# Five groups of elementwise work move from POOL to DVE, and transposes get 40 places of priority, in a one-core fp32 kernel of two transformer blocks

## The chip, the cores and the metric

The kernel runs on one core of one Trainium2 chip. A core has a matrix engine (PE), a vector engine (DVE), a scalar engine (ACT), a general engine (POOL) and a queue engine (SP), each of which takes its own instructions in the order in which they stand. The metric is the device time of one execution in microseconds (us), as the median of several runs; lower is better.

## The reference

The input is 512 tokens of width 1024 with a context of 256 tokens, all in fp32. Two blocks of two layers each run one after the other; the output is the tokens after the second.

```
# first block, each of two layers
h = rms_norm(x) * (1 + scale) + shift ;  p = h @ w_in ;  p_ctx = h_ctx @ w_in
layer 0: q, k = apply_rope(rms_norm(heads(p))), y_a = softmax attention over context and all tokens
         y_b = hyena_branch: two long convolutions with generated taps,
               taps = taps * rsqrt(sum(taps * taps, axis=0) + EPS)
layer 1: y_w = windowed attention (q, k with rope) ;  y_n = neighbourhood attention (8 x 16 keys per token)
y = concat(y_1 * silu(gate_1), y_2 * silu(gate_2)) ;  x = x + gate * (y @ w_out)

# second block, each of two layers
merged = sigmoid(x @ w_g0) * (o_nsa @ w_br_nsa) + sigmoid(x @ w_g1) * (o_mla @ w_br_mla)
       + sigmoid(x @ w_g2) * (o_fox @ w_br_fox)
x = layer_norm(a * x + merged @ w_out)
x = layer_norm(a * x + cross_attention(x, mem))
x = layer_norm(a * x + square(relu(x @ w_up)) @ w_down)

def apply_rope(x, cos, sin):      # pairs (x0, x1) of a head
    return stack([x0 * cs - x1 * sn, x0 * sn + x1 * cs])
```

## The kernel before

**Tiles.** Tokens stand in tiles of 128 rows. Every product that must be exact is made of three matmuls in the reduced form fp32r: each operand is split into a high and a low part (`split`, L54 on ACT writes the high part, L55 the low part, by a subtraction on DVE or on the engine that `eng` names), and `mm3` (L81 to L83) adds high x high, high x low and low x high in PSUM. Weights come by DMA to a staging tile and are split on their way into a tile `u` (`wu`, L1178).

**Transposes.** `tr` (L86) transposes a 128x128 block on PE through an identity matrix into the PSUM tag `pt`; ACT and DVE copy the result out and split it.

**Stages.** In the first block, `gqa_proj` projects q, k and v of an attention. Each pair of 128-token tiles goes through `head_norm`: a square on ACT (L255), sums of squares on DVE (L256), the inverse root in nine small DVE instructions (L63 to L76), the scaling (L259), and, where there is a rope, four strided products with the sine on POOL (L270), one product with the cosine on DVE (L272) and the sum of the two on DVE (L273), whose result PE transposes. In layer 0 this projection runs alone; in layer 1 it runs beside other work. The hyena filters' taps are made in `hy_taps`: the squares of a block (L549 on ACT) are added up (L550 on POOL) and summed over partitions by a matmul with ones (L555). `gates` multiplies an attention's output by silu of its gate: a tanh, a product on DVE out of PSUM (L757) and a product on POOL (L759). `nat_proj` (L898 on) projects for the neighbourhood attention and has its weights split on POOL (L902); `neigh` is that attention, where the probabilities are transposed, copied out by ACT (L1023) and multiplied with the values (L1026). `out_proj` adds its output on POOL (L778), which stays so.

In the second block, three attentions run beside the `branch` generator: a gate projection, a branch projection, a product on DVE out of PSUM (L1672) and, for the second and third branch, an addition to `merged` on POOL (L1673).

**Order.** Stages are generators; `mix` draws from two of them in turn, by the costs that they yield, so that attention and projections alternate in the program. A scheduler then sets each engine's order at build time: among instructions whose operands come in order it takes the one of the highest priority, which is the place in the program, unless a `high_priority` block moves it ahead by its offset. PSUM has two tiles of the tag `mm`, three of `S`, two of `pt` and one of `o`; in SBUF `u` and `st` have four tiles each, `e` six and `va` four.

In the names below, `e`, `a`, `u`, `sm` and so on are these tags; numbers behind them count the tiles.

Of the kernel before, what the change touches and what calls it, by code (L numbers as in the profile page):

```python
# [12 lines left out]
OP = mybir.AluOpType  # L13
AF = mybir.ActivationFunctionType
AX = mybir.AxisListType
P = 128
# [11 lines left out]
class Net:  # L28
# [54 lines left out]
        mm(ps, al, bh, start=False, stop=last)  # L83

    def tr(self, dst, src, n=P):
        self.nc.tensor.transpose(dst, src, self.ident[:n, :n])  # L86


    def q_pair(self, ps, A, B, n, scale=None):
# [158 lines left out]
    def head_norm(self, p, nh, gain, rope=None, tag='v2'):  # L248

        nc = self.nc  # L250
        n = 2 * nh * 64
        sq = self.t(tag, [P, 512])[:, :n]
        q = self.t(tag, [P, 512])[:, :n]
        ss = self.t('sm', [P, 2 * nh])
        nc.scalar.activation(sq.rearrange("p (i c) -> p i c", i=2), p, AF.Square)  # L255
        nc.vector.tensor_reduce(ss, sq.rearrange("p (h d) -> p h d", d=64), axis=AX.X, op=OP.add)  # L256
        r = self.rsqrt(ss, 2 * nh, 1.0 / 64, 1e-6).rearrange("p (i h) -> p i h", i=2)
        q4 = q.rearrange("p (i h d) -> p i h d", i=2, d=64)
        nc.vector.tensor_tensor(q4, p.rearrange("p i (h d) -> p i h d", d=64), bc(r[:, :, :, None], [P, 2, nh, 64]), op=OP.mult)  # L259
        if rope is None:  # L260
            q3 = q.rearrange("p (h d) -> p h d", d=64)
            nc.vector.tensor_tensor(q3, q3, bc(gain[:, None, :], [P, 2 * nh, 64]), op=OP.mult)
            return q
        cs, sn = rope
        qo = q.rearrange("p (i h c two) -> p i h c two", i=2, c=32, two=2)
        to = sq.rearrange("p (i h c two) -> p i h c two", i=2, c=32, two=2)
        so = sn.rearrange("p i (c two) -> p i c two", two=2)
        for i in range(2):
            for e in range(2):
                nc.gpsimd.tensor_tensor(to[:, i, :, :, e], qo[:, i, :, :, 1 - e], bc(so[:, i, None, :, e], [P, nh, 32]),  # L270
                                        op=OP.mult)
        nc.vector.tensor_tensor(q4, q4, bc(cs[:, :, None, :], [P, 2, nh, 64]), op=OP.mult)  # L272
        nc.vector.tensor_tensor(q, q, sq, op=OP.add)  # L273
        return q
# [240 lines left out]
    def hy_taps(self, o, hf, ni, w3, C):  # L515
# [13 lines left out]
        for b in range(nb):  # L529
            d = C['dec'][b // 2][:, b % 2, ch]  # L530
            ps = self.ps('S')
            for j in range(2):
                c = slice((b0 + b) * P, (b0 + b + 1) * P)
                p = ps[:, j * 256:(j + 1) * 256]
                nc.tensor.matmul(p, hs[:, c], wh[:, j, ch], start=True, stop=False)
                nc.tensor.matmul(p, hs[:, c], wl[:, j, ch], start=False, stop=b > 0)
                if b == 0:

                    for m in range(2):
                        for ww in (wh, wl):  # L540
                            nc.tensor.matmul(p, self.h0[:, (m + j + 1) % 2], ww[:, m, ch], start=False,
                                             stop=m == 1 and ww is wl)
            v = self.t('va', [P, 2, 256])
            nc.vector.tensor_tensor(v, ps.rearrange("p (j c) -> p j c", j=2), bc(d[:, None, :], [P, 2, 256]), op=OP.mult)
            if b == 0:
                nc.scalar.activation(acc, v, AF.Square)
            else:
                q = self.t('va', [P, 2, 256])
                nc.scalar.activation(q, v, AF.Square)  # L549
                nc.gpsimd.tensor_tensor(acc, acc, q, op=OP.add)  # L550
            self.split(E[b][:, 0], E[b][:, 1], v)
            yield 2.2
        ps = self.ps('o')[:, :256]
# [191 lines left out]
    def gates(self, w, i0, streams, order, fill=False):  # L745

        nc = self.nc
        for m in order:
            u = self.wu(w, i0 + m)
            for h, nt, y in streams:  # L750
                n = nt * P
                ps = self.ps('mm')[:, :n]
                self.pT(ps, u, h, slice(0, n))
                th = self.t('v2', [P, 512])[:, :n]
                nc.scalar.activation(th, ps, AF.Tanh, scale=0.5)
                yt = y[m // 2][:, m % 2]
                nc.vector.scalar_tensor_tensor(yt if fill else th, th, 1.0, ps, op0=OP.add, op1=OP.mult)  # L757
                if not fill:
                    nc.gpsimd.tensor_tensor(yt, yt, th, op=OP.mult)  # L759
                yield 5.2 * nt / 4  # L760

    def out_proj(self, w, y, nt, xs, gate, each):
# [134 lines left out]
    def nat_proj(self, streams, gain):  # L897

        nc = self.nc
        for i0, what in ((10, 'k'), (14, 'v'), (6, 'q')):  # L900
            for c in range(2):
                us = [self.wu('w1', i0 + 2 * c + k, eng=nc.gpsimd) for k in range(2)]  # L902
                cs = slice(c * 256, (c + 1) * 256)
                for h, nt, ctx in streams:
                    if what == 'q' and ctx:
# [745 lines left out]
    def branch(self, l, b, gi, o, x, merged, first=False):  # L1651
# [4 lines left out]
        for m in range(8):  # L1656
# [12 lines left out]
            if first:  # L1669
                nc.vector.scalar_tensor_tensor(d, g, 1.0, ps, op0=OP.add, op1=OP.mult)  # L1670
            else:
                nc.vector.scalar_tensor_tensor(g, g, 1.0, ps, op0=OP.add, op1=OP.mult)  # L1672
                nc.gpsimd.tensor_tensor(d, d, g, op=OP.add)  # L1673
            yield 5.2 + nk * .65

    def run(self, *gens):
# [539 lines left out]
```

## Time and profile before

| | |
|---|---|
| median of 3 runs | 2979.03 us (2976.75, 2979.03, 2984.97) |
| profiled run | 2982.7 us, of which the span is 2980.6 us |
| PE busy | 2817.7 us, 95% of the span |
| DVE busy | 1947.7 us, 65% |
| ACT busy | 1380.4 us, 46% |
| POOL busy | 262.4 us, 9% |
| TensorE's granted clock, mean | 0.982 of full speed |

The span runs from the first to the last instruction of the profiled execution; what lies around it is start and end of the run. Busy time is the time in which an engine had at least one instruction at work. A matmul's own time in a row is longer than the step to the next one, because matmuls overlap; the step is read from two starts. An idle time in square brackets stands before the row's instruction, with the instruction whose end ended it.

### The profile page before, as it was taken

The numbers are of one execution on the slowest core, as the hardware profiler recorded it, in microseconds if no ns is written. First come the engines' busy times: TensorE is split into PE (matmuls) and PEld (weight loads), VectorE is DVE, ScalarE is ACT, GpSimd is POOL, SyncE is SP. The second block draws the span as 40 slices with busy tenths as digits, with TensorE's granted clock in tenths as the row PEclk, the third lists the DMA queues.
The fourth block names the chain that finished last, engine by engine and source line by source line (L and its number), as shares of the span: only waits on it lengthen the run. The fifth ranks groups of instructions, "written<-read, shape, count | busy, mean of one in ns | idle before, by whom it ended". The sixth has DMA issues, their size and how long they took to land.

```text
span 2980.6 us, 40408 instructions
## 1 busy us (share of the span) xinstructions
PE 2817.7 (95%) x14904; PEld 2285.3 (77%) x14904; DVE 1947.7 (65%) x4339; ACT 1380.4 (46%) x2843; POOL 262.4 (9%) x310
## 2 busy tenths in 40 slices
PE   7898899889899899999999899999999999899998
PEld 3788757558888778777788788887787778788886
DVE  5767768885777756976756843436787663954335
ACT  5543566343365634655543522324465552633222
POOL 0212100101211310100110000000100011000000
PEclk8999999899999999999999999999999999999999
DMA  6433133653214332312124232323221124223221
GB/s 226 136 121 98 37 93 103 214 184 110 70 56 133 100 101 83 103 63 71 52 85 142 74 118 85 110 92 124 72 93 57 57 71 148 86 85 113 93 98 64
DMA packets 117645, 299.76 MB, mean 101 GB/s; under 512 B 21471, under 2 KB 48031, under 8 KB 117448
## 3 DMA queue, kind: packets, MB, share of 16 engines
q1 hardware_dynamic: 117448, 297.19, 30.8%
q8 instruction: 117, 1.92, 0.3%
q14 instruction: 80, 0.66, 0.1%
HBM read 273.54 MB, written 27.54 MB: 101 GB/s over the span
## 4 chain that ended last, share of the span: by engine, by line
PE 72%; DVE 15%; ACT 5%; issue 3%; DMA 1%; POOL 1%; SPq 0%; ACTq 0%; DVEq 0%; POOLq 0%
PE mm L81 17%; PE mm L82 17%; PE mm L83 17%; PE pt L86 5%; PE o L120 2%; DVE u L55 2%; PE o L121 2%; PE S L81 1%; PE S L83 1%; PE S L82 1%; PE mm L160 1%; PE o L1026 1%; PE o L160 1%; ACT u L54 1%; PE S L1632 1%
## 5 line engine op out<-in xcount | busy, mean ns | idle before, releaser
L81 PE MATMUL mm<-a,u 128*128 128x512 f32 (+1 forms) x1596 | 595.2, 374 | 6.7 <-ACT a L54 2.4
L82 PE MATMUL mm<-a,u 128*128 128x512 f32 (+1 forms) x1596 | 591.8, 371 | 0.8 <-DVE a L55 0.7
L83 PE MATMUL mm<-a,u 128*128 128x512 f32 (+1 forms) x1596 | 588.7, 370 | 0.4 <-DVE u L55 0.4
L54 ACT ACTIVATE u<-st 128x1024 fp32r<-128x1024 f32 x352 | 368.9, 1051 | 404.4 <-PE mm L83 338.0
L55 DVE TENSOR_TENSOR u<-st,u 128x1024 fp32r<-128x1024 f32 x340 | 431.2, 1268 | 133.6 <-ACT u L54 127.5
L81 PE MATMUL mm<-u,a 128*128 128x512 f32 (+1 forms) x1280 | 459.6, 359 | 9.6 <-DVE v L777 4.7
L82 PE MATMUL mm<-u,a 128*128 128x512 f32 (+1 forms) x1280 | 458.0, 358 | 3.8 <-DVE u L55 3.8
L83 PE MATMUL mm<-u,a 128*128 128x512 f32 (+1 forms) x1280 | 457.4, 357 | 0.0
L81 PEld LDWEIGHTS mm<-a,u 128*128 128x128 f32 x1596 | 301.7, 190 | 57.6 <-ACT a L54 4.3
L83 PEld LDWEIGHTS mm<-a,u 128*128 128x128 f32 x1596 | 301.8, 189 | 47.0 <-DVE u L55 0.8
L82 PEld LDWEIGHTS mm<-a,u 128*128 128x128 f32 x1596 | 301.8, 189 | 45.8 <-issue 1.4
L81 PEld LDWEIGHTS mm<-u,a 128*128 128x128 f32 x1280 | 243.1, 190 | 46.2 <-DVE v L777 5.0
L82 PEld LDWEIGHTS mm<-u,a 128*128 128x128 f32 x1280 | 243.5, 190 | 38.1 <-DVE u L55 4.9
L83 PEld LDWEIGHTS mm<-u,a 128*128 128x128 f32 x1280 | 243.1, 190 | 34.0 <-issue 0.2
L86 PE MATMUL pt<-c_ident,e 128*128 128x128 f32 x1132 | 189.8, 279 | 32.2 <-DVE e L273 9.4
L55 DVE TENSOR_TENSOR va<-pt,va 128x512 fp32r<-128x512 f32 (+2 forms) x252 | 164.5, 669 | 78.2 <-ACT va L54 76.4
L1206 DVE SCALAR_TENSOR_TENSOR a<-a,mm 128x512 f32<-128x512 f32 x96 | 65.7, 684 | 214.4 <-PE mm L83 214.3
L54 ACT ACTIVATE va<-pt 128x512 fp32r<-128x512 f32 (+2 forms) x252 | 141.5, 582 | 137.0 <-PE pt L86 131.5
L86 PEld LDWEIGHTS pt<-c_ident,e 128*128 128x128 f32 x1132 | 135.6, 142 | 76.9 <-issue 33.3
L1891 DVE TENSOR_TENSOR v<-v 128x512 f32<-128x512 f32 x64 | 44.3, 692 | 157.4 <-ACT v L1890 157.4
L1890 ACT ACTIVATE v<-mm 128x512 f32<-128x512 f32 x60 | 35.9, 599 | 200.4 <-PE mm L83 200.4
L82 PE MATMUL S<-u,a 128*128 128x256 f32 x312 | 90.2, 289 | 1.4 <-DVE u L55 1.4
(425 smaller groups left out, 4939.4 us busy)
## 6 DMA issues: line engine op xcount, KB each, us to landing
st<-in_up SPq DMA_DIRECT2D x64, 512.0 KB
st<-in_dn SPq DMA_DIRECT2D x64, 512.0 KB
st<-in_w SPq DMA_DIRECT2D x52, 512.0 KB
st<-in_ada SPq DMA_DIRECT2D x48, 512.0 KB
st<-in_gate SPq DMA_DIRECT2D x48, 512.0 KB
st<-in_win SPq DMA_DIRECT2D x42, 512.0 KB
st<-in_wout SPq DMA_DIRECT2D x24, 512.0 KB
st<-in_br SPq DMA_DIRECT2D x16, 512.0 KB
```

Of the source, the lines that this page charges most:

```text
L54: nc.scalar.activation(hi, src, AF.Copy)
L55: (eng or nc.vector).tensor_tensor(lo, src, hi.bitcast(F), op=OP.subtract)
L81: mm(ps, ah, bh, start=first, stop=False)
L82: mm(ps, ah, bl, start=False, stop=False)
L83: mm(ps, al, bh, start=False, stop=last)
L86: self.nc.tensor.transpose(dst, src, self.ident[:n, :n])
L120: nc.tensor.matmul(o, v, ph[:nk], start=first and bi == 0, stop=False)
L121: nc.tensor.matmul(o, v, pl[:nk], start=False, stop=last and bi == len(blocks) - 1)
L160: nc.tensor.matmul(ps[:nr], cc[:, 2 * kk + j], v[:, j * 512:(j + 1) * 512], start=kk + j + x == 0, stop=2 * kk + j == 7 and x == len(w) - 1)
L1206: self.nc.vector.scalar_tensor_tensor(xx, xx, alpha, ps, op0=OP.mult, op1=OP.add, **kw)
L1890: nc.scalar.activation(r, ps, AF.Relu)
L1891: nc.vector.tensor_tensor(sq, r, r, op=OP.mult)
```

## The change

Two things are changed. The transpose is issued under a priority of 40 places further ahead, so that the scheduler may take it before up to 40 instructions that stand before it in the program. And five groups of instructions run on DVE where they ran on POOL: the rope's products with the sine, the addition of the squares of the taps, the product with the gate, the subtraction in the weight split of `nat_proj`, and the addition of the second and third branch.

```diff
     def tr(self, dst, src, n=P):
-        self.nc.tensor.transpose(dst, src, self.ident[:n, :n])
+        with self.tc.high_priority(offset=40):
+            self.nc.tensor.transpose(dst, src, self.ident[:n, :n])
...
-                nc.gpsimd.tensor_tensor(to[:, i, :, :, e], qo[:, i, :, :, 1 - e], bc(so[:, i, None, :, e], [P, nh, 32]),
+                nc.vector.tensor_tensor(to[:, i, :, :, e], qo[:, i, :, :, 1 - e], bc(so[:, i, None, :, e], [P, nh, 32]),
                                         op=OP.mult)
...
-                nc.gpsimd.tensor_tensor(acc, acc, q, op=OP.add)
+                nc.vector.tensor_tensor(acc, acc, q, op=OP.add)
...
                 if not fill:
-                    nc.gpsimd.tensor_tensor(yt, yt, th, op=OP.mult)
+                    nc.vector.tensor_tensor(yt, yt, th, op=OP.mult)
...
-                us = [self.wu('w1', i0 + 2 * c + k, eng=nc.gpsimd) for k in range(2)]
+                us = [self.wu('w1', i0 + 2 * c + k) for k in range(2)]
...
-                nc.gpsimd.tensor_tensor(d, d, g, op=OP.add)
+                nc.vector.tensor_tensor(d, d, g, op=OP.add)
```

The line after L86 is new, so that every later line of the changed kernel has a number higher by one.

On DVE, at the last rotary of layer 1's window projection, before:

```order
L259 TENSOR_TENSOR e_1407_7196<-S_1405_7146,sm_1410_7202 128x512
L272 TENSOR_TENSOR e_1407_7196<-e_1407_7196,a_1328_6577 128x512
L757 SCALAR_TENSOR_TENSOR oa_1326_6574<-v2_1417_7263,mm_1416_7238 128x512
L273 TENSOR_TENSOR e_1407_7196<-e_1407_7196,e_1406_7195 128x512
L256 TENSOR_REDUCE sm_1421_7317<-e_1419_7315 128x8
```

and now:

```order
L260 TENSOR_TENSOR e_1407_7196<-S_1405_7146,sm_1410_7202 128x512
L758 SCALAR_TENSOR_TENSOR oa_1326_6574<-v2_1417_7263,mm_1416_7238 128x512
L271 TENSOR_TENSOR e_1406_7195<-e_1407_7196,a_1328_6577 128x128 x4
L55 TENSOR_TENSOR u_1465_7499<-st_1464_7497,u_1465_7499 128x1024
L273 TENSOR_TENSOR e_1407_7196<-e_1407_7196,a_1328_6577 128x512
L274 TENSOR_TENSOR e_1407_7196<-e_1407_7196,e_1406_7195 128x512
L96 TENSOR_TENSOR a_1376_6922<-pt_1426_7344,a_1376_6922 64x4x128
```

The four products of the rope and one weight split have come into DVE's row between the scaling and the sum that PE's transposes read; the product of the gate has moved ahead of them.

On PE, at the same place (`e_1407` is the operand that DVE finishes above), before:

```order
L82 MATMUL S_1418_7266<-u_1402_7141,a_1276_6345 128x256
L83 MATMUL S_1418_7266<-u_1402_7141,a_1280_6349 128x256
L86 MATMUL pt_1426_7344<-c_ident_149,e_1392_7095 128x128 x4
L86 MATMUL pt_1427_7353<-c_ident_149,e_1407_7196 128x128 x4
L393 MATMUL S_1432_7375<-a_1331_6586,a_1375_6921 128x256 x4
```

and now:

```order
L87 MATMUL pt_1426_7344<-c_ident_149,e_1392_7095 128x128
L81 MATMUL S_1418_7266<-u_1400_7136,a_1274_6343 128x256
L87 MATMUL pt_1426_7344<-c_ident_149,e_1392_7095 128x128 x3
L82 MATMUL S_1418_7266<-u_1400_7136,a_1274_6343 128x256
L83 MATMUL S_1418_7266<-u_1400_7136,a_1278_6347 128x256
L81 MATMUL S_1418_7266<-u_1400_7136,a_1274_6343 128x256
L82 MATMUL S_1418_7266<-u_1400_7136,a_1274_6343 128x256
L87 MATMUL pt_1427_7353<-c_ident_149,e_1407_7196 128x128 x4
L83 MATMUL S_1418_7266<-u_1400_7136,a_1278_6347 128x256
L81 MATMUL S_1418_7266<-u_1402_7141,a_1275_6344 128x256
```

The transposes of `e_1407` stood behind all matmuls of the projection `S_1418`; now 13 of these matmuls stand behind the transposes, of which the last two rows are the first.

On PE, in the neighbourhood attention (`e_1893` and `e_1904` are probabilities, `va_1898` the copy of the first one's transpose), before:

```order
L86 MATMUL pt_1897_9795<-c_ident_149,e_1893_9787 128x128 x4
L1007 MATMUL S_1943_9980<-a_1855_9642,a_1857_9644 128x256 x2
L1009 MATMUL S_1943_9980<-a_1858_9645,a_1857_9644 128x256 x2
L86 MATMUL pt_1908_9853<-c_ident_149,e_1904_9845 128x128 x4
L1026 MATMUL o_1835_9580<-va_1898_9800,a_1820_9521 64x128 x2
L1026 MATMUL o_1835_9580<-va_1898_9800,a_1822_9527 64x128 x2
```

and now:

```order
L87 MATMUL pt_1897_9795<-c_ident_149,e_1893_9787 128x128 x4
L1010 MATMUL S_1935_9947<-a_1858_9645,a_1857_9644 128x256
L82 MATMUL mm_2028_10308<-a_1277_6346,u_2027_10305 128x512
L83 MATMUL mm_2028_10308<-a_1273_6342,u_2027_10305 128x512
L81 MATMUL mm_2028_10308<-a_1273_6342,u_2027_10305 128x512
L1027 MATMUL o_1835_9580<-va_1898_9800,a_1820_9521 64x128 x2
L1027 MATMUL o_1835_9580<-va_1898_9800,a_1822_9527 64x128 x2
L82 MATMUL mm_2028_10308<-a_1277_6346,u_2027_10305 128x512
L1008 MATMUL S_1943_9980<-a_1855_9642,a_1857_9644 128x256 x2
L1010 MATMUL S_1943_9980<-a_1858_9645,a_1857_9644 128x256 x2
L87 MATMUL pt_1908_9853<-c_ident_149,e_1904_9845 128x128 x4
```

The first transposes have come ahead of the end of the score matmuls before them, and matmuls of a gate's projection (`mm_2028`) stand between them and the output matmul that reads their copy; the second transposes now stand behind that output matmul.

## Rows read from the trace of the kernel before

**Rows 1.** The page: span, and busy time, share and instructions by engine.

```profile
span 2980.6 us, 40408 instructions
...
PE 2817.7 (95%) x14904; PEld 2285.3 (77%) x14904; DVE 1947.7 (65%) x4339; ACT 1380.4 (46%) x2843; POOL 262.4 (9%) x310
```

**Rows 2.** Windows: PE, PEld, DVE, ACT, POOL busy us (instructions), clock, DMA.

```profile
1000.00:1100.00 100.00, 89.39 (x549) 71.80 (x548) 65.08 (x156) 53.22 (x105) 22.67 (x32) 0.98 0.28 89
...
1400.00:1500.00 100.00, 97.70 (x474) 75.58 (x475) 73.65 (x220) 58.36 (x161) 10.05 (x7) 1.00 0.19 60
```

**Rows 3.** Waits of PE, 265 to 345 us: total us, times, longest.

```profile
PE pt L86 <- DVE sm L63: 8.0, 3, 3.1
PE pt L86 <- DVE sm L66: 2.0, 1, 2.0
PE pt L86 <- DVE e L273: 1.9, 1, 1.9
```

**Rows 4.** Waits of PE over the whole span.

```profile
PE o L1026 <- ACT va L1023: 6.6, 13, 0.8
...
PE o L555 <- POOL ec L550: 4.7, 4, 1.8
```

**Rows 5.** Groups on POOL: count | busy us, mean ns | idle before, releaser.

```profile
L1673 POOL TENSOR_TENSOR a<-a,v 128x512 f32<-128x512 f32 x32 | 45.3, 1415 | 312.6 <-DVE v L1672 244.9 <-DVE sma L1588 49.4 <-DVE sma L1643 18.2
...
L55 POOL TENSOR_TENSOR u<-st,u 128x1024 fp32r<-128x1024 f32 x12 | 29.5, 2464 | 103.9 <-ACT u L54 59.9 <-issue 44.0
L550 POOL TENSOR_TENSOR ec<-ec,va 128x512 f32<-128x512 f32 x16 | 24.1, 1509 | 115.9 <-ACT va L549 92.4 <-issue 23.4
...
L270 POOL TENSOR_TENSOR e<-e,a 128x128 f32<-128x128 f32 x32 | 17.2, 571 | 63.6 <-DVE e L259 63.6
...
L759 POOL TENSOR_TENSOR oa<-oa,v 128x512 f32<-128x512 f32 x12 | 15.8, 1320 | 217.1 <-DVE v L757 203.2 <-DVE sma L413 13.9
```

**Rows 6.** Groups on DVE, 1700 to 2000 us, where POOL is empty.

```profile
L55 DVE TENSOR_TENSOR u<-st,u 128x1024 fp32r<-128x1024 f32 x56 | 68.6, 1225 | 20.4 <-ACT u L54 18.8
```

**Rows 7.** Instructions by time at 298 us: start, us, engine, line, tiles [idle before].

```profile
298.28 0.69 DVE L272 TENSOR_TENSOR e<-e,a 128x512 f32<-128x512 f32 x1 [1.82 <-POOL e L270]
...
299.49 0.68 DVE L273 TENSOR_TENSOR e<-e,e 128x512 f32<-128x512 f32 x1
...
300.31 0.63 PE L86 MATMUL pt<-c_ident,e 128*128 128x128 f32 x4 [3.08 <-DVE sm L63]
```

**Rows 8.** Groups on DVE over the whole span: a product of 128x128.

```profile
L293 DVE TENSOR_TENSOR a<-a,gn 128x128 f32<-128x128 f32 x8 | 2.1, 280 | 0.0
```

**Rows 9.** Instructions by time at 783 us, the last rotary of layer 1.

```profile
783.30 0.28 PE L82 MATMUL S<-u,a 128*128 128x256 f32 x1
...
783.42 0.28 PE L83 MATMUL S<-u,a 128*128 128x256 f32 x1
...
784.03 1.91 POOL L270 TENSOR_TENSOR e<-e,a 128x128 f32<-128x128 f32 x4 [6.52 <-DVE e L259]
...
785.91 5.09 POOL L55 TENSOR_TENSOR u<-st,u 128x1024 fp32r<-128x1024 f32 x2
785.98 2.81 DVE L272 TENSOR_TENSOR e<-e,a 128x512 f32<-128x512 f32 x1 [2.09 <-POOL e L270]
...
788.72 0.67 DVE L757 SCALAR_TENSOR_TENSOR oa<-v,mm 128x512 f32<-128x512 f32 x1
789.31 2.23 DVE L273 TENSOR_TENSOR e<-e,e 128x512 f32<-128x512 f32 x1
...
791.69 1.09 PE L86 MATMUL pt<-c_ident,e 128*128 128x128 f32 x4 [7.54 <-DVE e L273]
```

**Rows 10.** Who waited for POOL's line 270: us, times.

```profile
  DVE e L272: 19.8, 12
```

**Rows 11.** Instructions of PE by time at 1117 us, transposes of a new x.

```profile
1116.97 0.39 PE L81 MATMUL mm<-a,u 128*128 128x256 f32 x1 [0.25 <-ACT a L54]
...
1118.19 0.63 PE L86 MATMUL pt<-c_ident,a 128*128 128x128 f32 x4 [0.30 <-DVE a L55]
```

## The prediction

> **What bounds the kernel now.** I read the busy lines of the page first [rows 1]: PE is busy for 2817.7 of 2980.6 us, DVE for 1947.7, POOL for 262.4. So PE is the bound over the whole span, and the 163 us in which it is idle are the most that a better order could give back; DVE and POOL matter only where PE waits for them. Then I read the windows [rows 2], because the 95% is an average. From 1400 to 1500 us, where the attention of the second block runs beside its gated branches, PE is busy 97.70 of 100 us although DVE is at 73.65 and POOL at 10.05: nothing on POOL or DVE is late for long there. From 1000 to 1100 us, where the neighbourhood attention has run out of projection matmuls, PE is busy only 89.39. Last I read who ended PE's waits: the attention projections of the first block's layer 0, between 265 and 345 us [rows 3], wait 8.0 + 2.0 + 1.9 = 11.9 us for DVE; over the whole span [rows 4] the tap norm waits 4.7 us for POOL, and the output matmuls of the neighbourhood attention 6.6 us, in 13 waits, for ACT's copy of the transposed probabilities.
>
> The sum is made on the profiled run: 2982.7 us, of which the span is 2980.6. The median of the three runs is 2979.0, 3.7 us or 0.12% less; I carry the differences over to the median as they are. About 0.3%, 9 us, is what a measurement can tell from no change.
>
> **Part one, POOL to DVE: the work.** Five groups leave POOL [rows 5]: 32 merge adds at 1.415 us, 12 halves of weight splits at 2.464, 16 tap-norm adds at 1.509, 48 rotary products (32 of them 128x128 at 0.571) and 20 gate products (12 of them 128x512 at 1.320). On DVE the split costs 1.225 us where POOL is empty [rows 6], a product of 128x512 about 0.68 (that form at line 273, [rows 7]), one of 128x128 0.280 [rows 8]; the smaller forms I take at half of the next larger. Together: 12 x 1.225 = 14.7, 32 x 0.68 = 21.8, 16 x 0.68 = 10.9, 12 x 0.68 + 8 x 0.34 = 10.9, 32 x 0.28 + 16 x 0.14 = 11.2, in all 69.5 us. If DVE got nothing back it would go from 65% to 68% of the span, still far under PE.
>
> It does get something back. At 785.98 us line 272, a product of two operands in SBUF, takes 2.81 us, and line 273 at 789.31 takes 2.23 [rows 9], where the same forms take 0.69 and 0.68 at 298 and 299 us [rows 7]. What is different is POOL: two weight splits run there from 785.91 for 5.09 us. The product of line 757 between them reads PSUM and keeps its 0.67. So those two splits cost DVE (2.81 - 0.69) + (2.23 - 0.68) = 3.7 us, 1.85 for each 2.5 us on POOL.
>
> **A. The last rotary of layer 1's window projection.** PE stands idle for 7.54 us before the transposes at 791.69 [rows 9], which read the product of line 273. On DVE of the changed kernel the order there is: line 758 (0.67), four rotary products (4 x 0.28 = 1.12), one weight split (1.22), lines 273 and 274 (0.69 + 0.68), 4.4 us in all, from about 783.9, when POOL could start before (784.03). So the operand is there at 788.3 instead of 791.5, 3.2 us earlier. But the transposes now stand 13 rows ahead in PE's order, and 13 score matmuls at 0.12 us (783.30 to 783.42) come after them that before ran in front of the wait: 1.6 us go back. **-1.6 us.** Bounds: with both splits in front -0.4, with none in front -2.8.
>
> **B. The other eleven rotaries.** DVE sat idle 19.8 us in 12 waits for POOL's rotary [rows 10]; on DVE the same work is 11.2 us, so DVE's chain is shorter by 8.6 us, some 0.7 us a rotary. PE's waits of [rows 3] are the same places: at 300.31 it waits 3.08 us for transposes whose operand line 273 writes at 299.49, and line 272 before it had waited 1.82 us for POOL [rows 7]. Six of the twelve belong to layer 0 and stand there, worth 6 x 0.7 = 4.3 us if all of it is on PE's path. Against it, in the changed order these transposes stand 15 to 19 rows further ahead inside the score matmuls, which then end 15 to 19 x 0.12 = 1.8 to 2.3 us later after each wait, and the next norm starts from them. I take half of the gain, **-2.1 us**; bounds -4.3, and +9 when four of the five waits of [rows 3] pay 2.3 us in full.
>
> **C. Tap norm.** The matmul of line 555 waits for POOL's add 4.7 us in 4 waits [rows 4]. The add falls from 1.51 to 0.68 us, 0.8 each or 3.3 in four, but it now queues on DVE behind what stands there. **-2.5 us**, from 0 to -4.7.
>
> **E. Merge adds, gate products, the other weight splits.** They have PE's matmuls as cover: between 1400 and 1500 us PE is 97.7% busy [rows 2]. The 21.8 us of merge adds go to a DVE that has some 26 us of idle time in each 100 us there. If that cover were gone, each add would cost its 0.68 us. I take **0**, from -2 to +3 (four adds that are met by an empty PE).
>
> **Part two, the transposes.** It costs no work: the same 1652 transposes run. Followed by name through both orders, 606 stand earlier in PE's order and 540 later, because in the attention stages the whole attention stream slips 10 to 30 rows behind the projections; the mean is 0.9 row earlier.
>
> **D. Transposes at the head of a projection.** Where eight blocks of a new x are transposed [rows 11], matmuls and transposes alternate in waits of 0.25 and 0.30 us for the splits of the transposed blocks, 0.55 us in all. In the changed order these transposes stand 23 to 37 rows ahead, among matmuls that need nothing. The pattern stands at three places in each layer of the second block; those after a layer norm don't move. Six groups at 0.5: **-3 us**, from 0 to -6 (the same again where a second half follows).
>
> **F. Neighbourhood attention.** In the changed order the transposes stand 17 to 24 rows ahead in the mean (28 at most) between 960 and 1000 us, and projection matmuls are left over for the stretch after 1000 us, between a transpose and the output matmul that waits for its copy [rows 4]. Of the 6.6 us I take a third back: **-2 us**. The lower bound is all of it, -6; the upper is +4, since in places the output matmul now follows its transpose directly and may wait there 0.8 us, the longest of those waits, five times.
>
> Sum: -1.6 - 2.1 - 2.5 + 0 - 3 - 2 = -11.2 us. From 2979.0 that is **2968 us**, 0.38% faster.
>
> **The rivals.** *Hidden.* PE is at 95%, the terms are small and each hangs on one queue; with half of them taken elsewhere 5 us are left, and if the slips of the attention stream undo D and F too, less: 2974 to 2979. For it speaks that 606 against 540 is hardly a move at all; against it, that A and C are waits whose ends can be followed row by row.
>
> *Slower: PE blocked by its own transposes.* A transpose placed ahead of its operand holds the matmuls behind it; in the trace none runs in the 7.54 us before 791.69 [rows 9]. The price: 12 rotary tails, each some 18 rows ahead at 0.12 us, are 2.2 us each; if each is paid as idle time, 26 us. Less A, C and D (7.1 us) and the 8.6 us by which DVE's chain is shorter, this is +10.3: 2989 us, and 3005 if nothing is gained against it. It decides from the point where PE's waits for DVE between 265 and 345 us pass some 25 us instead of 11.9. For it: DVE, not PE, sets the pace there. Against it: DVE is ahead by 0.7 us a rotary, and in the second block nearly all operands are there when PE comes. The Trainium skill, page "TensorE: Matmul & The Clock Gate", section "The mechanism", says that matmuls keep strict order in start and end, so that nothing behind a waiting transpose passes it. By that rule the price is paid wherever the operand is late, and the trace agrees at 791.69.
>
> *Better than forecast: the contention is everywhere.* If POOL stretches DVE's instructions at more places than the one I followed, DVE is ahead everywhere in the first block: B at -4.3 for both layers (-8.6), C at -4.7, F at -6, D at -6, A at -1.6: 2979 - 27 = 2952. For it: by the 1.85 us for each split above, the five rows of [rows 5], 131.9 us of POOL time, could hold back DVE by up to 98 us, more than the 69.5 it takes on. Against it: PE waits for DVE only 11.9 us where I looked, and most products that are met read PSUM. The Trainium skill, page "SBUF — State Buffer", section "Who interferes with whom", says that a DVE instruction with two SBUF inputs contends with a GpSimd one that reads SBUF, and calls the shared port pair an exclusive lock. A whole lock of the two splits would be 2 x 2.46 = 4.9 us instead of the 3.7 read, so the trace agrees in kind and falls short in size.
>
> **How the numbers follow.** Forecast 2968, from 2960 to 2972: 0.32. Better, 2950 to 2960: 0.13. Hidden, 2972 to 2988: 0.32. Slower, 2988 to 3005: 0.23. Under 2970.1 it is faster by over 0.3%: the better case and 0.28 of the forecast, 0.41. Within: 0.04 + 0.32 = 0.36. Over 2988: 0.23. The range from 2952 to 2996 leaves out half of the slower case and a quarter of the better one, 0.15 in all.
>
> **What the changed profile would show.** A: lines 273 and 274 at about 786 us at 0.69 us, and PE's transposes of that place at 788 to 789. B: no waits of DVE for POOL at line 273, PE's waits between 265 and 345 us under 11. C: no wait of line 556 for POOL, and less than 2.2 us for DVE. D and F: PE busier from 1000 to 1100 us than 89.4. DVE's busy time should be between 1920 and 2017 us (98 back, or nothing), the likelier the nearer to 1975. PE idle at transposes for more than 25 us in all between 265 and 345 us, or the time from 2000 us on longer than before, would prove me wrong.

## The result, and the profile after

The changed kernel takes 2933.53 us, the median of four runs (2931.91 to 2934.67), against 2980.64 for the kernel before: a ratio of 0.9841, 95% interval 0.9824 to 0.9858, 47 us faster. A second set of runs, on one chip with other kernels, gave 2931.57 against 2981.42, 0.9837 (0.9822 to 0.9852). The forecast was 2968 with a range down to 2952, so the direction was right and the size was a quarter of what came. The profiled run of the changed kernel took 2934.61 us.

The page of the changed kernel, its span and its busy lines, against [rows 1]:

```profile
span 2932.8 us, 40392 instructions
...
PE 2795.8 (95%) x14904; PEld 2278.0 (78%) x14904; DVE 1974.4 (67%) x4467; ACT 1383.5 (47%) x2843; POOL 124.6 (4%) x182
```

Three things are to be seen. PE runs the same 14904 matmuls and is busy 21.9 us less. DVE has taken over work that I priced at 69.5 us and is busy only 26.7 us more, so some 43 us of its time came back. POOL has lost 137.8 us.

The windows of the changed kernel (columns as in [rows 2]); the program stands 22 us earlier by 600 us and 38 us earlier by 1000 us, so a window holds slightly later work than the same window of before:

```profile
500.00:600.00 100.00, 87.21 (x350) 59.36 (x349) 95.32 (x138) 43.09 (x65) 13.89 (x6) 0.95 0.58 197
700.00:800.00 100.00, 95.36 (x677) 89.64 (x676) 87.47 (x288) 45.40 (x96) 0.00 (x0) 0.98 0.28 84
1000.00:1100.00 100.00, 94.55 (x571) 78.91 (x570) 54.39 (x107) 40.57 (x69) 15.24 (x16) 1.00 0.29 98
1400.00:1500.00 100.00, 99.94 (x473) 79.53 (x473) 68.92 (x173) 52.83 (x126) 0.00 (x0) 1.00 0.21 66
```

and two windows of the kernel before that I had not shown and should have read:

```profile
500.00:600.00 100.00, 86.50 (x344) 58.09 (x342) 84.17 (x115) 33.87 (x48) 11.89 (x8) 0.90 0.54 179
700.00:800.00 100.00, 89.34 (x588) 81.70 (x587) 74.75 (x197) 40.98 (x76) 23.63 (x27) 0.97 0.28 93
```

In these two stages PE was not covered: it was busy for 86.5 and 89.3 us of 100 while DVE was at 84 and 75, and POOL, at 12 and 24, still worked beside DVE. From 500 to 600 us the granted clock was 0.90.

To see where the 47 us arose, each matmul of a run is looked up in the run before by its place in the program. The table gives, for the matmuls that started in 50 us from the given time of the run before, how many us earlier (negative) or later they start, as the median, in the profiled run of each kernel. The columns are described with the experiments below. A profiled run can lie off its kernel's median, and its column with it: the splits' lies 6 us below theirs, the priority's 5 and the moves' 9.5, so these columns end at -19, -12 and -48 us where the medians say -12.8, -4.1 and -37; the column for the shadow lies 3 us above.

```
us of    rope  split   gate   taps  merge  prio.  moves  after  shadow  memset
before  alone  alone  alone  alone  alone  alone  alone
  250     1.0   -1.1   -0.9   -6.3    0.1   -1.4   -6.1   -3.9    -0.5    -3.4
  400    -1.5   -1.1   -2.5   -6.0    1.1   -5.0  -10.1   -9.6    -6.0    -9.6
  500    -2.3   -1.2   -2.7   -6.1    1.0   -1.4  -17.1  -14.7   -11.0   -14.3
  550    -7.4   -1.0   -9.8   -5.7   -0.3    2.1  -25.0  -23.6   -19.0   -23.2
  700    -7.3   -1.8  -10.3   -7.4   -1.8    1.8  -25.6  -21.8   -15.7   -22.7
  800   -12.0   -8.2  -10.6   -7.6   -0.6    2.9  -37.0  -30.1   -19.9   -30.5
 1000   -13.1  -15.7  -13.1   -9.6   -0.6   -2.7  -41.8  -37.8   -22.8   -36.9
 1300   -13.3  -16.3  -13.6   -9.7   -1.0   -5.4  -42.4  -37.5   -22.6   -37.0
 2000   -13.9  -17.1  -14.1   -9.9   -3.3   -9.1  -45.6  -42.4   -25.9   -41.1
 2900   -12.4  -19.1  -14.3   -8.4   -5.6  -11.9  -48.4  -47.5   -28.8   -46.2
```

The changed kernel has 38 of its 47 us by 1000 us, all in the first block: 4 in the filters' taps, 11 from there to 500 us, 7 to 9 between 500 and 600, 8 between 700 and 800, and 8 more up to 1000. The second block, which is two thirds of the span, gives the other 10.

### The profile page after: what moved, and what is told of

The parts are those of the page before. It is cut to its first block, busy times and chain, and to the rows that moved or that the text cites. A ratio compares the mean times of both kernels' runs of the same rounds, so it can differ in the third digit from the quotient of the medians.

```text
span 2932.8 us, 40392 instructions
## 1 busy us (share of the span) xinstructions
PE 2795.8 (95%) x14904; PEld 2278.0 (78%) x14904; DVE 1974.4 (67%) x4467; ACT 1383.5 (47%) x2843; POOL 124.6 (4%) x182
## 4 chain that ended last, share of the span: by engine, by line
PE 75%; DVE 15%; ACT 5%; issue 2%; DMA 2%; SPq 0%; POOL 0%; ACTq 0%; DVEq 0%
PE mm L82 17%; PE mm L81 17%; PE mm L83 17%; PE pt L87 6%; DVE u L55 2%; PE o L121 2%; PE o L122 2%; PE o L161 1%; PE S L83 1%; PE S L81 1%; PE S L82 1%; PE mm L161 1%; PE o L1027 1%; DVE a L55 1%; PE S L1633 1%
```

## The experiments

All are timed against the kernel before on the same chip. "Alone" is one part of the change put into the kernel before.

### The two halves of the change

The priority alone:

```diff
-        self.nc.tensor.transpose(dst, src, self.ident[:n, :n])
+        with self.tc.high_priority(offset=40): self.nc.tensor.transpose(dst, src, self.ident[:n, :n])
```

> The kernel before with the transposes' 40 places of priority alone. Theory 1 (the gain of 47 us comes from the five moves: POOL no longer stretches DVE's instructions, and DVE's chains are shorter): 2972 to 2988 us, no change. Theory 2 (the gain comes from the order: transposes stand earlier, so their copies are ready when PE asks): 2935 to 2950 us.

The five moves alone, which are the diff ahead of the prediction without the one of `tr`:

> The kernel before with the five moves from POOL to DVE alone, transposes at their own priority. Theory 1: 2930 to 2945 us. Theory 2: 2970 to 2985 us. If the two parts only work together, both this run and the one with the priority alone stay over 2960 us.

The priority alone took 2976.38 us, 0.9984 (0.9975 to 0.9993): 4 us. The moves alone took 2943.53, 0.9866 (0.9844 to 0.9888): 37 us, with runs from 2934.04 to 2947.88. So theory 1 holds in the main: the moves are the gain. The priority is worth 4 us by itself and some 10 on top of the moves (2943.5 to 2933.5); the runs of the moves spread over more than that, and the fastest of them, the profiled one, is as fast as the changed kernel.

PE's waits between 263 and 345 us with the priority alone:

```profile
PE pt L86 <- DVE sm L63: 4.5, 1, 4.5
PE pt L86 <- DVE e L273: 3.6, 3, 2.1
PE pt L86 <- DVE sm L66: 3.1, 1, 3.1
PE pt L86 <- DVE e L262: 1.0, 1, 1.0
```

These are 12.2 us at transposes, where before had 11.9 [rows 3]. Transposes 15 to 19 rows further ahead neither cost nor gave anything there.

### The rope alone, and the weight splits alone

```diff
-                nc.gpsimd.tensor_tensor(to[:, i, :, :, e], qo[:, i, :, :, 1 - e], bc(so[:, i, None, :, e], [P, nh, 32]),
+                nc.vector.tensor_tensor(to[:, i, :, :, e], qo[:, i, :, :, 1 - e], bc(so[:, i, None, :, e], [P, nh, 32]),
```

> The kernel before with the rope's products alone on DVE. Theory 1, its half on shorter chains: PE's waits between 265 and 345 us fall from 11.9 us to about 7 and the wait of 7.5 us at 791 shrinks to 3 to 5 us, 2965 to 2975 us in all; the contention is left as it was. Theory 2: 2975 to 2985 us.

```diff
-                us = [self.wu('w1', i0 + 2 * c + k, eng=nc.gpsimd) for k in range(2)]
+                us = [self.wu('w1', i0 + 2 * c + k) for k in range(2)]
```

> The kernel before with the weight splits of the neighbourhood projection alone on DVE. If the moves add up one by one (the five moves gave 37 us, the rope 11.4 of them), this one gives the gain between 760 and 1000 us that the rope does not: 2968 to 2974 us. If they only work together, 2976 to 2984 us.

The rope alone took 2969.11 us, 0.9954 (0.9940 to 0.9969), 11.4 us faster; the splits alone 2969.33, 0.9954 (0.9939 to 0.9968), 12.8 us faster. The rope came out as theory 1 had it, and the splits in the first of their two ranges. The two meet at the last rotary of layer 1, the place of [rows 9], and show who held whom there. With the splits alone on DVE (instructions in order of time):

```profile
783.49 0.69 DVE L272 TENSOR_TENSOR e<-e,a 128x512 f32<-128x512 f32 x1 [1.52 <-POOL e L270]
784.10 1.22 DVE L55 TENSOR_TENSOR u<-st,u 128x1024 fp32r<-128x1024 f32 x1
785.24 0.68 DVE L273 TENSOR_TENSOR e<-e,e 128x512 f32<-128x512 f32 x1
...
786.07 1.09 PE L86 MATMUL pt<-c_ident,e 128*128 128x128 f32 x4 [3.71 <-DVE e L273]
```

Lines 272 and 273 are back at 0.69 and 0.68 us, though the rope is still on POOL, and PE's wait is 3.71 us instead of 7.54. With the rope alone on DVE:

```profile
776.16 2.34 POOL L55 TENSOR_TENSOR u<-st,u 128x1024 fp32r<-128x1024 f32 x1 [1.40 <-ACT u L54]
776.75 2.51 DVE L270 TENSOR_TENSOR e<-e,a 128x128 f32<-128x128 f32 x4
...
781.33 1.09 PE L86 MATMUL pt<-c_ident,e 128*128 128x128 f32 x4 [4.47 <-DVE e L273]
```

The four products meet POOL's split and take 2.51 us; in the changed kernel they take 0.90 (below). So at this place both halves of the theory are seen: a shorter chain, and a neighbour on POOL that holds DVE up.

### The gate products alone, and the tap-norm adds alone

```diff
-                    nc.gpsimd.tensor_tensor(yt, yt, th, op=OP.mult)
+                    nc.vector.tensor_tensor(yt, yt, th, op=OP.mult)
```

> The kernel before with the gate products alone on DVE. Adding up: a gain between 480 and 560 us and again between 780 and 1000 us, 2970 to 2976 us. Only together: 2976 to 2984 us.

```diff
-                nc.gpsimd.tensor_tensor(acc, acc, q, op=OP.add)
+                nc.vector.tensor_tensor(acc, acc, q, op=OP.add)
```

> The kernel before with the tap-norm adds alone on DVE. Adding up: PE's 4 waits for POOL's add (4.7 us) go and DVE's instructions beside them are no longer stretched, a gain before 270 us: 2974 to 2978 us. Only together, or the add queues on DVE: 2978 to 2985 us.

The gate products alone took 2967.96 us, 0.9954 (0.9937 to 0.9971), 14.2 us faster, the largest of the five and more than expected; half of it arises from 500 to 550 us in the table, and between 800 and 1000 us there are only 2.5 of it. Just ahead of that step the kernel before shows

```profile
509.50 1.67 POOL L759 TENSOR_TENSOR oa<-oa,v 128x512 f32<-128x512 f32 x1 [11.60 <-DVE v L757]
...
510.27 1.45 DVE L700 TENSOR_TENSOR a<-e,e 128x512 f32<-128x512 f32 x1
```

a product of the hyena's convolution that takes 1.45 us beside POOL's gate, where its form takes 0.69, on a DVE that is 84% busy. And the window from 530 to 560 us of the kernel before:

```profile
530.00:560.00 30.00, 26.93 (x92) 15.32 (x91) 19.88 (x28) 12.60 (x18) 0.00 (x0) 0.77 0.64 204
```

beside the same one with the gate products alone on DVE:

```profile
530.00:560.00 30.00, 26.16 (x111) 16.72 (x110) 24.57 (x36) 14.44 (x19) 0.00 (x0) 0.94 0.85 299
```

PE runs 111 matmuls instead of 92 there, and its granted clock is 0.94 instead of 0.77. So part of the gain is PE's clock: the half speed level (1.2 GHz) stood for 13.7 us from 540.0 us in the kernel before, after PE had waited 2.1 us in three pieces since 530, and for 3.4 us, from 552.8 us, in this one.

The tap-norm adds alone took 2973.98 us, 0.9973 (0.9962 to 0.9984), 8.2 us faster; 6.3 of it are there between 250 and 300 us. PE's waits for POOL's line 550, 4.7 us in [rows 4], are gone, and only 1.3 us came in their place (PE's waits for line 649 on DVE, 2.3 us before and 3.6 now); and beside the adds, DVE's splits of the taps had been stretched. That group on DVE, 0 to 260 us, in the kernel before (count | busy us, mean ns):

```profile
L55 DVE TENSOR_TENSOR u<-va,u 128x512 fp32r<-128x512 f32 x16 | 14.9, 930 | 5.9 <-ACT u L54 5.9
```

and with the adds on DVE:

```profile
L55 DVE TENSOR_TENSOR u<-va,u 128x512 fp32r<-128x512 f32 x16 | 10.9, 684 | 2.1 <-ACT u L54 2.1
```

### The merge adds alone

```diff
-                nc.gpsimd.tensor_tensor(d, d, g, op=OP.add)
+                nc.vector.tensor_tensor(d, d, g, op=OP.add)
```

> The kernel before with the merge adds alone on DVE. Adding up: 2 to 4 us between 1300 and 1550 and as much between 2250 and 2450 us: 2974 to 2978 us. Covered by PE, as the prediction had it: 2978 to 2984 us, and these stretches keep their length.

2977.78 us, 0.9985 (0.9975 to 0.9994), 4.4 us faster, at the edge of both expectations. The stretch of the merge adds in the kernel before and, below it, with the adds on DVE:

```profile
1350.00:1550.00 200.00, 197.53 (x931) 154.60 (x930) 129.69 (x341) 102.39 (x252) 21.97 (x28) 1.00 0.21 68
```

```profile
1350.00:1550.00 200.00, 199.74 (x941) 156.51 (x940) 134.53 (x355) 101.49 (x249) 3.43 (x15) 1.00 0.20 70
```

PE is busy 2.2 us more here, and by the table the adds bring 2.7 us between 1000 and 2000 us and 2.3 more by 2900. For these adds, the cover that the prediction named was nearly whole.

The five alone give 11.4 + 12.8 + 14.2 + 8.2 + 4.4 = 51 us, together 37. They do not add up one by one: the same wait or dip of the clock goes away by more than one of them.

### POOL busy again, with reads and without

If the gain is that POOL no longer competes with DVE for operands in SBUF, then work on POOL that nobody waits for must bring the loss back. In the changed kernel, beside each moved add, product and split (the rope's apart):

```diff
+    def shadow(self, x, n):
+        m = -(-n // 222)
+        for k in range(m):
+            c = slice(k * n // m, (k + 1) * n // m)
+            self.nc.gpsimd.tensor_tensor(self.dummy[:, :c.stop - c.start], x[:, c], x[:, c], op=OP.mult)
...
                 nc.vector.tensor_tensor(acc, acc, q, op=OP.add)
+                self.shadow(q.rearrange('p j c -> p (j c)'), 512)
...
                     nc.vector.tensor_tensor(yt, yt, th, op=OP.mult)
+                    self.shadow(th, n)
...
+                for u_ in us:
+                    self.shadow(u_[0].bitcast(F), 1024)
...
                 nc.vector.tensor_tensor(d, d, g, op=OP.add)
+                self.shadow(g, 512)
```

> The changed kernel, and beside each tap-norm add, gate product, weight split and merge add that moved to DVE, POOL again works for about as long on the same operands into a tile that nobody reads (two to five pieces each, written as bf16). If contention with POOL for DVE's SBUF operands is a large part of the 47 us, 20 to 40 us come back: 2953 to 2973 us. If the gain is the shorter chains or the order alone, 2932 to 2940 us.

2950.57 us: 17 to 19 us of the gain are gone, a little less than the 20 that I had set for a large part. But these instructions also wait and hold buffers. The control keeps them and takes the reads away:

```diff
     def shadow(self, x, n):
-        m = -(-n // 222)
-        for k in range(m):
-            c = slice(k * n // m, (k + 1) * n // m)
-            self.nc.gpsimd.tensor_tensor(self.dummy[:, :c.stop - c.start], x[:, c], x[:, c], op=OP.mult)
+        self.nc.gpsimd.tensor_copy(self.dummy[:, :1], x[:, :1])
+        for k in range(n // 64):
+            self.nc.gpsimd.memset(self.dummy, 0.0)
```

> The control to the run with the doubled POOL work: the changed kernel with the same places of extra POOL work, but this copies one column of the operand and then only writes zeros for about as long, so that POOL is busy and reads next to nothing. If the 17 us of that run are contention for what DVE reads in SBUF, they are not here: 2931 to 2938 us. If they come from the added instructions, their waits and the buffers that they hold: 2945 to 2955 us.

2936.23 us, 4.7 above the changed kernel in the same set of runs. That also speaks against a rival, that an emptier POOL serves the work left on it sooner: here POOL is busier than in the kernel before (368.7 us against 262.4), and only 4.7 us go. The busy lines of the two, first with reads, then with memsets:

```profile
PE 2811.5 (95%) x14904; PEld 2286.3 (77%) x14904; DVE 1996.2 (68%) x4467; ACT 1384.3 (47%) x2843; POOL 312.6 (11%) x438
```

```profile
PE 2799.7 (95%) x14904; PEld 2280.0 (78%) x14904; DVE 1973.0 (67%) x4467; ACT 1384.1 (47%) x2843; POOL 368.7 (13%) x966
```

DVE runs the same 4467 instructions. Beside a POOL that reads it is busy for 1996.2 us, beside a POOL that is busier still but mostly writes for 1973.0, which is the changed kernel's 1974.4. So the reads alone stretch DVE by 23 us, and 2950.6 - 2936.2 = 14.3 us reach the end (15 when each is set against the kernel before on its own chip). Contention is shown as a cause. The shadow works 191 us on POOL, against 121 us of the four groups of before that it stands for; at that share the loss of before would be 14.3 x 121 / 191, some 9 us, an estimate.

That estimate is a low one, because the shadow works in short pieces (0.53 us in the median for those of a weight split, where the split held POOL for 2.46). Counted in the traces, 73 DVE instructions of the kernel before take over 0.1 us longer than their form does elsewhere, every one beside a POOL instruction, 66 us in all; beside the four groups it is 40.5 us (splits 14.8, merge adds 11.0, tap adds 9.0, gate products 5.7), and in the changed kernel 31 us of the 66 are left. The shadow stretches DVE by only 24.5 us with its 191. By stretched time the loss of before would be 14.3 x 40.5 / 24.5, some 24 us. Between 9 and 24 the runs do not decide. The rope's products on POOL stretched no DVE instruction, so that its 11.4 us come from the shorter chain.

Two more runs ask the same of one move at a time, in the kernel before: the splits on DVE with POOL's shadow of them, and the gate products on DVE with theirs.

```diff
-                us = [self.wu('w1', i0 + 2 * c + k, eng=nc.gpsimd) for k in range(2)]
+                us = [self.wu('w1', i0 + 2 * c + k) for k in range(2)]
+                for u_ in us:
+                    self.shadow(u_[0].bitcast(F), 1024)
```

> The kernel before with the neighbourhood projection's weight splits on DVE (12.8 us faster alone), and POOL again reading each split's high part, in five pieces, into a tile that nobody reads: POOL is as busy as before, and DVE does the split. If that gain is contention, it goes: 2975 to 2985 us. If it is the shorter way from a weight's arrival to its split, it stays: 2966 to 2972 us.

```diff
-                    nc.gpsimd.tensor_tensor(yt, yt, th, op=OP.mult)
+                    nc.vector.tensor_tensor(yt, yt, th, op=OP.mult)
+                    self.shadow(th, n)
```

> The kernel before with the gate products on DVE (14.2 us faster alone), and POOL again working on the tanh's tile after each. If that gain is contention: 2975 to 2985 us. If it is the shorter chain from the gate to the output projection, and fewer dips of PE's clock between 530 and 600 us: 2966 to 2973 us.

The splits with their shadow took 2972.22 us, 9.4 faster than before instead of 12.8; the gates with theirs 2973.34, 8.2 instead of 14.2. Both fell between the two expectations: a quarter and some two fifths of the gain go with the shadow's contention. But these are lower bounds: the splits' shadow stretches DVE by 5.3 us where the splits on POOL did by 14.8, and the gates' by 2.8 where the products did by 5.7. Scaled by that, contention would be some 9.5 of the 12.8 us and 12 of the 14.2, an estimate. In the run with the gates' shadow PE's half speed at 540 us is back as well, 13.7 us as in the kernel before, so part of its loss comes through the clock. That the larger part is the shorter chain is thus not shown for these two.

### More of the same

The changed kernel and the add of `out_proj` on DVE as well:

```diff
-                nc.gpsimd.tensor_tensor(xs[i][:, sl], xs[i][:, sl], v, op=OP.add)
+                nc.vector.tensor_tensor(xs[i][:, sl], xs[i][:, sl], v, op=OP.add)
```

> The changed kernel, and the output projection's add, the longest group left on POOL, on DVE as well. If each move off POOL goes on paying: 2924 to 2931 us. If it queues on DVE, where DVE already ends PE's waits from 540 to 600 us: 2933 to 2942 us.

The changed kernel with 80 places:

```diff
-        with self.tc.high_priority(offset=40):
+        with self.tc.high_priority(offset=80):
```

> The changed kernel with 80 places of priority for the transposes instead of 40. If transposes further ahead of their operands block PE: 2938 to 2950 us, with longer waits of PE at transposes between 260 and 330 us. If the place hardly matters, as the run with the priority alone (4 us) says: 2930 to 2938 us.

Both of these together:

> The changed kernel with the output projection's add on DVE and 80 places of priority together; alone they gave 2.4 and 1.5 us, hardly more than the runs differ. Adding up: 2927 to 2930 us. If both were chance: 2931 to 2935 us.

And with two more groups on DVE:

```diff
-            for j, (eng, op) in enumerate(((nc.vector, OP.add), (nc.gpsimd, OP.subtract))):
+            for j, (eng, op) in enumerate(((nc.vector, OP.add), (nc.vector, OP.subtract))):
...
-                nc.gpsimd.tensor_tensor(bias[:, v].rearrange("p (r c) -> p r c", c=32),
+                nc.vector.tensor_tensor(bias[:, v].rearrange("p (r c) -> p r c", c=32),
```

> As the run before, and the last two groups of SBUF arithmetic on POOL, the hyena taps' difference and the neighbourhood bias, on DVE too, so that POOL is left with the adaptive gates' add, casts, copies and memsets. If POOL beside DVE is a price wherever it reads SBUF: 2922 to 2928 us. If these two had cover: 2928 to 2934 us.

> The changed kernel once more, beside the three others on one chip: 2930 to 2936 us; the dips of the clock differ from run to run, so some microseconds between runs are no difference.

With the add of `out_proj` 2931.08 us, with 80 places 2931.98, both no clear difference to the changed kernel's 2931.57 to 2933.53. Together 2926.69 (2925.22 to 2928.20), and with everything 2924.09 us (2916.45 to 2924.98), 0.9804 (0.9790 to 0.9819): 7.5 us better than the changed kernel on the same chip, and the fastest of all here. 80 places cost nothing either: the rival of transposes that block PE has no run that speaks for it.

## Why the prediction was wrong

**The bound.** PE is the bound, and the windows show it before and after. But "the 163 us in which it is idle are the most that a better order could give back" is wrong: idle time fell from 163 to 137 us, 26 us, and the other 22 came out of PE's busy time, with the same number of matmuls. Time at half speed counts as busy, so the column hides it (from 530 to 560 us PE is busy 26.93 us for 92 matmuls at a clock of 0.77, and 26.16 for 111 at 0.94); I have not divided the 22 us further.

**E, the step that failed.** "They have PE's matmuls as cover: between 1400 and 1500 us PE is 97.7% busy", hence 0. That window holds merge adds alone. The gate products stand between 330 and 530 us and again from 967 to 1003, the weight splits between 768 and 923, and I took the cover of one stage for them all. Alone, splits, gates and merge adds give 12.8, 14.2 and 4.4 us; the last is the one whose window I had read, and it came nearest to 0. What the step took for covered was in PE's way: the splits and gate products while on POOL stretched DVE's own instructions by 20.5 us, in stages where PE waits for DVE.

**A** said -1.6 us. The changed kernel's rows at the place:

```profile
759.45 0.69 DVE L260 TENSOR_TENSOR e<-S,sm 128x512 f32<-128x512 f32 x1
760.06 0.68 DVE L758 SCALAR_TENSOR_TENSOR oa<-v,mm 128x512 f32<-128x512 f32 x1
760.65 0.90 DVE L271 TENSOR_TENSOR e<-e,a 128x128 f32<-128x128 f32 x4
...
761.46 1.22 DVE L55 TENSOR_TENSOR u<-st,u 128x1024 fp32r<-128x1024 f32 x1
...
762.60 0.69 DVE L273 TENSOR_TENSOR e<-e,a 128x512 f32<-128x512 f32 x1
763.32 0.69 DVE L274 TENSOR_TENSOR e<-e,e 128x512 f32<-128x512 f32 x1
...
764.16 1.09 PE L87 MATMUL pt<-c_ident,e 128*128 128x128 f32 x4 [3.35 <-DVE e L274]
```

DVE's chain is much as worked out: the steps after the scaling, which I put at 4.4 us, take 3.95 us from 760.06 to 764.01, and of the durations only that of the four products was too long (0.90, not 1.12). PE's wait is 3.35 us instead of 7.54, where my sum gives 7.54 - 3.2 + 1.6 = 5.9. The whole stage from 700 to 800 us gave 8.3 us: beside this place, PE's other waits for DVE between 760 and 830 us of before, 2.0 and 1.7 us, have no counterpart between 745 and 800 us now, and the clock is at half speed for 3.4 us from 764.0 instead of 6.8 from 789.1.

**B** said -2.1. PE's waits between 260 and 335 us now, against [rows 3]:

```profile
PE pt L87 <- DVE sm L63: 3.7, 1, 3.7
PE S L394 <- DVE e L260: 1.6, 2, 1.4
PE pt L87 <- DVE e L263: 0.7, 1, 0.7
PE pt L87 <- DVE sm L66: 0.4, 1, 0.4
PE pt L87 <- DVE e L274: 0.3, 1, 0.3
```

At transposes they are 5.1 us instead of 11.9, so the gain is over the 4.3 us that I gave as its bound, and the price of the rows ahead, for which I took half away, was not paid. The rope alone has it at 6.4 us there without any change of rows. As forecast, DVE waits for POOL no more at line 273.

**C** said -2.5, from 0 to -4.7; alone the adds give 8.2. The waits for POOL went whole, and the stretched splits of the taps (16 x 0.25 us), which I had not priced, came on top.

**D and F** said -5 together, and the priority alone gives 4.1 us. In its column the step from 800 to 1000 us, -5.6, is the neighbourhood attention, and -2.7 follow up to 1300. That fits the two terms in size, but this profiled run is the fastest of ten, 5 us under their median, and its column stands at +2.9 us at 800, so that each gave what it was put at is not shown. The sign that I named is there with the priority alone, where the program stands only 3 us earlier: the window of [rows 2] from 1000 to 1100 us has PE at 95.45 us instead of 89.39.

```profile
1000.00:1100.00 100.00, 95.45 (x571) 75.11 (x570) 67.47 (x155) 53.10 (x104) 26.33 (x34) 1.00 0.31 101
```

**DVE's work.** 1974.4 us is the value that I named as the likeliest, 1975. What I did with it was wrong: I let DVE's 43 us back reach PE only at the places followed by hand.

**The rivals.** "Better than forecast: the contention is everywhere" had the mechanism, with 0.13 of the chance. Its price, 27 us, was too small: it kept E at 0 and had no term for the clock. Against it I had set that most products that are met read PSUM; yet 73 stretched instructions stood in the trace, and I had followed two. "Slower" did not show, and of "Hidden" only the merge adds are a case.

**The clock, which the prediction left out.** The mean granted clock is 0.982 for the kernel before, the median of the 48 runs beside the experiments, and 0.985 and 0.9865 for the changed one, the medians of its two sets of four. One minus that, times the span, is the time that PE's half speed costs where PE has work: 54 us before, 44 and 40 after, so 10 to 14 of the 47 to 50 us are counted there. The third decimal is worth 3 us. The gate products alone bring it to 46, the rope to 49, the splits to 52; the tap adds, the merge adds and the priority leave it at 54 to 57. The dips follow stretches in which PE waits, as at 540 us; the moves shorten the waits, so I take this part for a consequence of the others and not a fourth cause; no run holds the clock fixed. Why the moves alone have it between 32 and 50 us from run to run stays open.

Summed up: contention 9 to 24 us (two estimates from the pair of runs with and without reads), the order of the transposes 4 to 10, and the rest the shorter chains through DVE, of which the rope's is shown, with 10 to 14 us of all this seen as clock. The parts overlap, and the runs don't divide them more sharply.

## What to carry to other kernels

Read the cover of each moved group in the window in which that group runs, and where engines meet, in the instructions by time; a stage that is 98% full says nothing of the next one. Small work on POOL beside a busy DVE is paid twice, by the way there and back and by the DVE instructions that stand beside it, so it belongs on DVE even when DVE is the busier engine, as long as PE waits for DVE's chain. A test for it: let POOL write beside the kernel, then read, and compare.

## What the runs showed of the hardware

At the places read here, DVE instructions with two operands in SBUF that started into a POOL instruction reading SBUF were held until that one had ended. POOL's two splits of [rows 9], taken one at a time:

```profile
785.91 2.34 POOL L55 TENSOR_TENSOR u<-st,u 128x1024 fp32r<-128x1024 f32 x1
788.20 2.79 POOL L55 TENSOR_TENSOR u<-st,u 128x1024 fp32r<-128x1024 f32 x1
```

They end at 788.25 and 790.99 us, and lines 272 and 273 end at 788.79 and 791.54, 0.54 and 0.55 us later, where the same forms take 0.69 us with no neighbour. Line 700 at 510 us ends 0.55 us after the gate product as well. The prediction held a whole lock of 4.9 us against the 3.7 read; that was a misreading, since a lock costs only what is left of POOL's instruction: 2.27 and 1.68 us were left when lines 272 and 273 started, each of which then took 0.55 us more instead of 0.69, which gives the 3.7. The Trainium skill, page "SBUF — State Buffer", section "Who interferes with whom", calls the shared port pair an exclusive lock, and says that a GpSimd instruction which only writes does not contend with DVE's second input. Both agree with the traces: lines 272 and 273 end only after POOL's splits, and DVE's busy time is 1973.0 us beside memsets, 1996.2 beside reads. Beside the added memsets 14 DVE instructions are stretched, by 1.8 us in all, each with a single tensor operand (`TENSOR_SCALAR`), and none with two.

Also small instructions are held. In the kernel before (instructions in order of time):

```profile
795.16 2.39 POOL L55 TENSOR_TENSOR u<-st,u 128x1024 fp32r<-128x1024 f32 x1 [4.17 <-ACT u L54]
795.18 2.39 DVE L67 TENSOR_SCALAR sm<-sm 128x8 int32<-128x8 int32 x1
797.49 0.16 DVE L68 TENSOR_SCALAR sm<-sm 128x8 f32<-128x8 f32 x1
```

An instruction of 128x8 with one operand takes 2.39 us beside POOL's split, and its like 0.16 us right behind it. The inverse root of a head's norm is a chain of thirteen small instructions (L63 and L66 to L68 once, L74 to L76 three times; the nine are the loop alone), so a split on POOL stretches it as well.

The clock differs between runs of one kernel: the shortest span of the kernel before, 2973.7 us, had 0.984, the longest, 2983.5, had 0.979. By one minus the clock, times the span, that is 15 us, more than the 10 us between the two spans.
